# Forty-four stores of a two-layer mixer block issued by ScalarE instead of SyncE

## The chip, the cores and the metric

The kernel runs on one core of one Trainium2 chip. The metric is the device time of one execution in microseconds (us), given as the median of several runs. One further execution is recorded by the hardware profiler, and every row shown here comes from that one.

The core has five instruction streams that matter: TensorE (PE in the rows, with PEld for its weight loads), VectorE (DVE), ScalarE (ACT), GpSimd (POOL) and SyncE (SP). Each works through its own list in order. A "q" behind an engine's name (SPq, ACTq) stands for its sequencer: waits, branches and the issue of transfers (DMAs), which are not counted as busy time.

## The reference, cut to what matters

Two layers (DEPTH 2) of a block on 1024 tokens x of width 1024 beside 256 context tokens. Each layer normalises, projects by `w_in` (1024 x 3856), runs four token mixers on 256 columns each, gates, multiplies by `w_out` and adds to the input. All is float32.

```
h = rms_norm(x, g_pre[l]) * (1 + scale) + shift ; p = h @ w_in[l]        # context alike
a: retention, two directions, 4 heads:   scores = (q k^T) * decay ; o ; head norm ; * silu(z)
b: spatial gating: gelu(u) * (w_s layer_norm(gelu(v)) + b_s) * silu(z)
c: short convolution: b * conv3(c * h) * silu(z)
d: gated delta rule, two directions, 4 heads, chunks of 64:
   q,k,v = silu(conv3(.)) ; q,k l2-normalised ; g = -exp(a_log)*softplus(a + dt) ; beta = sigmoid(b)
   gc = cumsum(g) in a chunk ; decay = exp(gc_i - gc_j)
   (I + lower(k k^T * decay * beta)) u = [v beta, k beta exp(gc)]        # triangular solve
   chunk after chunk: state update and output ; o * rsqrt(mean o^2) * norm_g * silu(z)
x = x + gate * rms_norm(concat(a, b, c, d) @ w_out[l], g_post[l])
```

## The kernel before, in words

Projections are done in three products (high and low halves of both operands) on TensorE. A piece of weights is loaded by SP (`halves`, L507), its high half is cast by ScalarE (`whi`, L511) and its low half is taken by GpSimd (`wlo`, L512), and then TensorE multiplies (`fm_products`, L607 to L609). The next piece of weights is prepared while the present one is multiplied.

Each layer (`run`) first does the gates of the delta rule (`gates`), then walks through its serial stages: `delta_keys`, `lanes`, `delta_queries`, `invert`, `delta_values`, `delta_solve`, `delta_steps`, `delta_out`. Between the steps of these, `beside` puts portions of independent work, a generator of projections and of the other mixers (`fillers`), so that TensorE has something to do while a serial stage waits. `drain` runs the rest of the generator.

Some tensors go through device memory to change their layout. All of these transfers are issued by SP in the kernel before:

- `gates`, L1017: the cumulated gates, turned by TensorE and copied by ScalarE (`ga`), are stored as decay rows `gc`. `delta_keys` (L1077) then loads them spread over partitions into `gR`, 32 loads in all.
- `delta_keys`, L1097: the token-major keys (`gkt`, copied from PSUM by ScalarE) are stored to `ktd`; `delta_solve` loads them back much later.
- `delta_queries`, L1162: the queries (`gp`, a Silu of ScalarE) are stored to `qd`; `delta_out` loads them back.
- `spread`, L778 and L781: the rows of the retention's head norm (`frow`, made by two activations of ScalarE in `rsqrt`, L361 and L362) are stored to `rfd` in four or eight small pieces and loaded back over partitions (L785).
- `delta_gate`, L1502: the Silu of the gate projection (`gz`) is stored to `gzd` in blocks, and `delta_out` loads it (L1482).

The order of the instructions on each engine isn't the order of the code. The framework (a tile scheduler) draws it when the kernel is built, from dependencies, priorities and its own estimates of when an operand is there; it also sets the waits. `after` adds an edge for that order alone, without a wait at run time:

```
self.tc.add_manual_dep(ins.ins, anchor.ins.name, LATER, reason="order")
```

So a transfer that goes to another engine's list can also move other instructions in the lists. In `lanes`, L1186 and L1192, a large relayout through device memory stands next to the stores of the queries. `affine_select` in `delta_keys` (L1082) runs on GpSimd, in the same list as `wlo`.

Of the kernel before, what the change touches and what calls it, by code (L numbers as in the profile page):

```python
# [19 lines left out]
P = 128  # L20
D = 1024
KC = 8
TL = 1024
TC = 256
T = TL + TC
# [68 lines left out]
class Block:  # L94
# [30 lines left out]
    def cst(self, c, n, r=slice(None)):  # L125

        o = max(x for x in self.csts if x <= c)
        return self.csts[o][1][r, c - o:c - o + n]
# [642 lines left out]
    def spread(self, rows, blocks, nm, pool, behind=None):  # L771

        nc = self.nc
        self.uid += 1
        d = self.dp.tile([2, T], F32, name=f"{nm}d{self.uid}")
        for g in range(4):
            if len(blocks) > 1:
                self.after(nc.sync.dma_start(d[:, :TL].rearrange("h (b g i) -> g h b i", b=2, g=4)[g],  # L778
                                             rows[32 * g:32 * g + 2, :256].rearrange("h (b i) -> h b i", b=2)), behind)
            if blocks[-1][0] == TL:  # L780
                self.after(nc.sync.dma_start(d[:, TL + 64 * g:TL + 64 * g + 64], rows[32 * g:32 * g + 2, 256:320]), behind)  # L781
        n = blocks[-1][0] + blocks[-1][1]
        o = self.slot(nm, pool)
        for hh in range(2):
            nc.sync.dma_start(o[64 * hh:64 * hh + 64, :n], d[hh:hh + 1, :n].to_broadcast([64, n]))  # L785
        return o
# [170 lines left out]
    def gates(self, l):  # L957

        nc, cst = self.nc, self.cst
        V = nc.vector  # L960
        tri = self.slot("tri", "G")[:, :C_N - C_TRI]
        self.after(nc.sync.dma_start(tri, self.a["cst"][:, C_TRI:]), self.have_mv)
        w = self.slot("ga", "G")
        x, e, u, ln_, den = (w[:, 160 * j:160 * j + 160] for j in range(5))
        x3 = x.rearrange("p (t k) -> p t k", k=16)
        na = self.small([P, 8], "na", 1)
        V.tensor_tensor(x3[:, :, :8], self.ab[:, :, :8], self.gv[:, 0, l].unsqueeze(1).to_broadcast([P, NT, 8]), ALU.add)
        V.tensor_scalar(x3[:, :, 8:], self.ab[:, :, 8:], -1.0, None, ALU.mult)
        self.log_exp(V.scalar_tensor_tensor(e, x, -1.0, x, ALU.mult, ALU.min))
        have_e = nc.scalar.activation(e, e, AF.Exp)  # L970

        V.tensor_scalar(u, e, 1.0, None, ALU.add)
        nc.scalar.activation(ln_, u, AF.Ln)
        V.tensor_scalar(u, u, -1.0, None, ALU.add)
        V.tensor_scalar(den, u, 0.0, None, ALU.is_equal)
        V.tensor_tensor(ln_, ln_, den, ALU.add)
        V.tensor_tensor(den, u, den, ALU.add)
        V.reciprocal(den, den)
        V.tensor_tensor(ln_, ln_, den, ALU.mult)
        V.tensor_tensor(e, ln_, e, ALU.mult)  # L980
        V.scalar_tensor_tensor(x, x, 0.0, e, ALU.max, ALU.add)
        self.after(nc.scalar.activation(na, self.gv[:, 1, l], AF.Exp), have_e)
        g = w[:, 800:880].rearrange("p (t k) -> p t k", k=8)
        V.scalar_tensor_tensor(g, x3[:, :, :8], -1.0, na.unsqueeze(1).to_broadcast([P, NT, 8]), ALU.mult, ALU.mult)

        pv = self.ps("vt")
        for d in range(2):
            nc.tensor.matmul(pv[:, 40 * d:40 * d + 40], lhsT=tri[:, 128 * d:128 * d + 128], rhs=g[:, :, 4 * d:4 * d + 4],
                             start=True, stop=True)
            nc.tensor.matmul(pv[:, 80 + 80 * d:160 + 80 * d], lhsT=tri[:, 256 + 128 * d:384 + 128 * d], rhs=g,  # L990
                             start=True, stop=True)

        vt = self.held("vtok", [P, NT, 24])
        self.eg = self.held("gexp", [P, NT, 8])
        gk = w[:, 880:960].rearrange("p (k t) -> p k t", t=NT)
        for d in range(2):
            p = pv[:, 40 * d:40 * d + 40].rearrange("p (t h) -> p t h", h=4)
            V.tensor_copy(vt[:, :, 4 * d:4 * d + 4], p)
            nc.scalar.copy(gk[:, 4 * d:4 * d + 4].rearrange("p h t -> p t h"), p)
        V.tensor_scalar(vt[:, :, 16:24], x3[:, :, 8:], -1.0, None, ALU.mult)  # L1000
        for q in range(2):
            r = slice(64 * q, 64 * q + 64)
            V.tensor_tensor(vt[r, :, 8:16], pv[r, 80 + 80 * q:160 + 80 * q].rearrange("p (t k) -> p t k", k=8), vt[r, :, 0:8], ALU.subtract)
        V.tensor_tensor(vt[:, :, 8:16], vt[:, :, 8:16], vt[:, :, 16:24], ALU.add)
        nc.scalar.activation(self.eg, vt[:, :, 0:8], AF.Exp)
        self.vtok = vt

        self.ec = self.held("gec", [P, 2, NT, 8])
        nc.scalar.activation(self.ec.rearrange("p q t k -> p (q t k)"), pv[:, 80:240], AF.Exp)

        pt = self.ps("gcT")
        nc.tensor.transpose(pt[:80, :P], w[:, 880:960], self.ident)
        gr = w[:80, 960:1088]
        self.have_eg = nc.scalar.copy(gr, pt[:80, :P])
        self.uid += 1
        self.gcd = [self.dp.tile([8, T], F32, name=f"gc_{self.uid}")]
        nc.sync.dma_start(self.gcd[0].rearrange("k (t i) -> (k t) i", i=P), gr)  # L1017

    def big(self, cols, nm, bufs=1):
        self.uid += 1  # L1020
# [38 lines left out]
    def delta_keys(self, l):  # L1059

        nc, cst = self.nc, self.cst
# [26 lines left out]
        for hp, k in enumerate(ks):  # L1088
            kt, sq = self.slot("gkt", "G"), self.slot("gks", "G")
            for t0, m in BLOCKS[True]:  # L1090
                self.beside(0.5, 1.5)
                pt = self.ps("gkT")
                for i in range(0, m, P):
                    nc.tensor.transpose(pt[:, i:i + P], k[:, t0 + i:t0 + i + P], self.ident)
                nc.scalar.copy(kt[:, t0:t0 + m], pt[:, :m])
                nc.scalar.activation(sq[:, t0:t0 + m], pt[:, :m], AF.Square)
            nc.sync.dma_start(self.ktd[hp], kt[:, :T])  # L1097
            last = V.tensor_reduce(kk[:, 0, :, 2 * hp:2 * hp + 2], sq[:, :T].rearrange("p (t h d) -> p t h d", h=2, d=64), AX.X, ALU.add)
        lk, self.sk = kk[:, 0], kk[:, 1]
        self.log_exp(last)  # L1100
# [43 lines left out]
    def delta_queries(self, l, ctx):  # L1144

        nc, cst = self.nc, self.cst
        V = nc.vector
        n = T if ctx else TL
        nt = n // P
        qs = self.delta_need(0)  # L1150
        D4 = self.D4

        def use_a(p, h, ts_):
            for d in range(2):
                V.tensor_tensor(D4[d][:, h, ts_], p, D4[d][:, h, ts_], ALU.mult)

        self.uid += 1
        self.qd = self.dp.tile([2, P, T], F32, name=f"qd{self.uid}")
        self.Ad = self.dp.tile([2, P, NT, 4, 64], F32, name=f"Ad{self.uid}")
        pq = self.ps("gq2")  # L1160
        for hp in range(2):
            nc.sync.dma_start(self.qd[hp, :, :n], qs[hp][:, :n])  # L1162
            q2 = self.slot("gq2", "G")
            nc.scalar.activation(q2[:, :n], qs[hp][:, :n], AF.Square)
            for t in range(nt):
                nc.tensor.matmul(pq[:, 20 * hp + 2 * t:20 * hp + 2 * t + 2], lhsT=q2[:, t * P:t * P + P],
                                 rhs=cst(C_INDQ, 2), start=True, stop=True)
            self.gram(self.qkv[1][hp], qs[hp], hp, range(nt), use_a)
        self.fq = self.held("gfq", [P, NT, 4])
        for hp in range(2):  # L1170
            nc.scalar.copy(self.fq[:, :nt, 2 * hp:2 * hp + 2], pq[:, 20 * hp:20 * hp + 2 * nt].rearrange("p (t h) -> p t h", h=2))
        for d in range(2):
            for h in range(4):
                self.after(nc.sync.dma_start(self.Ad[d][:, :nt, h], D4[d][:, h, :nt]), self.have_nl)
# [317 lines left out]
    def delta_gate(self, l, ctx):  # L1492

        nc = self.nc
        self.uid += 1
        zd = self.dp.tile([2, P, T], F32, name=f"gzd{self.uid}")
        for hp in range(2):
            z = self.slot("gz")

            def ev(b, t0, m):  # L1500
                nc.scalar.activation(z[:, t0:t0 + m], b, AF.Silu)
                nc.sync.dma_start(zd[hp, :, t0:t0 + m], z[:, t0:t0 + m])  # L1502

            yield from self.proj_fm(l, 14 * 256 + hp * P, BLOCKS[ctx], ev)
        self.gz = zd
# [181 lines left out]
```

## Time and profile before

| what | value |
|---|---|
| median of 3 runs | 1469.44 us (1469.21 to 1475.08) |
| profiled execution, its own time | 1477.17 us |
| its span, first to last instruction | 1475.4 us |
| mean granted TensorE clock | 0.961 of full speed |
| TensorE busy | 1378.5 us (93%) |
| VectorE, ScalarE, GpSimd busy | 741.5, 450.3, 325.9 us |
| mean DMA traffic | 113 GB/s |

The span leaves out 1.77 us of the profiled execution's own time. Busy time is the union of an engine's instructions; a wait or an issue on a sequencer is not part of it. The table of waits names, for each idle stretch of an engine, the instruction that stood next and what it waited for.

### The profile page before, as it was taken

To read this page: it belongs to the slowest core of one execution; us is meant where nothing else is said; L and a number is where in the kernel's file an instruction comes from. 1 tells how busy PE (TensorE), PEld (TensorE's weight loads), DVE (VectorE), ACT (ScalarE), POOL (GpSimd) and SP (SyncE) were. 2 spreads that over 40 slices of the span, in tenths; PEclk is the share of its full clock that TensorE was granted. 3 is DMA by queue.
4 is the path that set the end of the run, shared out by engine and by line. 5 is a ranking of instruction groups with operands and counts; after the bars stand their busy time and mean duration, and the time that the engine had idled before them with its cause. 6 is when DMAs were issued, how large, how long until landed. Compare 5 with 4: busy or idle time off the path is not lost.

```text
span 1475.4 us, 36425 instructions
## 1 busy us (share of the span) xinstructions
PE 1378.5 (93%) x15928; PEld 1156.9 (78%) x15928; DVE 741.5 (50%) x1385; ACT 450.3 (31%) x930; POOL 325.9 (22%) x265
## 2 busy tenths in 40 slices
PE   5799999799999999999999997997899999999997
PEld 4688788666787777789999985886667867878997
DVE  2477596333335727241555466393553576634232
ACT  5545422121101222322555535312111112333221
POOL 1123231113102211032222035111222112123220
PEclk9899899799999999999999998996999999999999
DMA  9505656126313212373334144644233004136351
GB/s 289 171 16 130 134 142 161 40 88 236 113 58 98 76 51 68 94 246 104 102 123 143 51 94 116 136 111 113 64 113 116 23 27 127 58 108 208 114 180 56
DMA packets 235849, 166.00 MB, mean 113 GB/s; under 512 B 112070, under 2 KB 205610, under 8 KB 235690
## 3 DMA queue, kind: packets, MB, share of 16 engines
q1 hardware_dynamic: 235690, 163.67, 38.3%
q8 instruction: 125, 2.05, 0.6%
q14 instruction: 34, 0.28, 0.1%
HBM read 123.39 MB, written 40.24 MB: 111 GB/s over the span
## 4 chain that ended last, share of the span: by engine, by line
PE 72%; DVE 11%; issue 7%; ACT 4%; DMA 3%; POOL 2%; SPq 0%; DVEq 0%; POOLq 0%; ACTq 0%
PE pj L607 13%; PE pj L608 12%; PE pj L609 12%; PE po L1578 4%; PE po L1580 4%; PE po L1579 4%; PE pt L599 3%; PE pt L601 2%; PE pt L600 2%; PE gu L1368 2%; DVE lt L1210 1%; PE ro L926 1%; POOL wlo L512 1%; PE ip L1253 1%; PE iq L1242 1%
## 5 line engine op out<-in xcount | busy, mean ns | idle before, releaser
L512 POOL TENSOR_TENSOR wlo<-raw,whi 128x512 fp32r<-128x512 f32 (+3 forms) x158 | 217.0, 1388 | 845.9 <-ACT whi L511 719.3
L607 PE MATMUL pj<-h0h,whi 128*128 128x512 f32 (+1 forms) x532 | 211.3, 397 | 8.8 <-ACT whi L511 6.0
L609 PE MATMUL pj<-h0h,wlo 128*128 128x512 f32 (+1 forms) x532 | 203.5, 383 | 3.1 <-POOL wlo L512 3.1
L608 PE MATMUL pj<-h0l,whi 128*128 128x512 f32 (+1 forms) x532 | 203.8, 383 | 0.0
L607 PE MATMUL pj<-h1h,whi 128*128 128x512 f32 (+1 forms) x532 | 203.4, 382 | 0.0
L608 PE MATMUL pj<-h1l,whi 128*128 128x512 f32 (+1 forms) x532 | 199.2, 374 | 0.0
L609 PE MATMUL pj<-h1h,wlo 128*128 128x512 f32 (+1 forms) x532 | 198.2, 373 | 0.1
L1578 PE MATMUL po<-wo,whi 128*128 128x256 f32 x576 | 163.5, 284 | 2.0 <-DVE hf L1604 1.5
L1580 PE MATMUL po<-wo,wlo 128*128 128x256 f32 x576 | 162.0, 282 | 0.8 <-POOL wlo L512 0.8
L1579 PE MATMUL po<-wo,whi 128*128 128x256 f32 x576 | 161.7, 281 | 0.0
L607 PEld LDWEIGHTS pj<-h0h,whi 128*128 128x128 f32 x532 | 104.6, 197 | 29.5 <-ACT whi L511 6.1
L609 PEld LDWEIGHTS pj<-h0h,wlo 128*128 128x128 f32 x532 | 104.0, 196 | 22.3 <-POOL wlo L512 3.8
L608 PEld LDWEIGHTS pj<-h0l,whi 128*128 128x128 f32 x532 | 104.3, 196 | 19.0 <-issue 3.2
L609 PEld LDWEIGHTS pj<-h1h,wlo 128*128 128x128 f32 x532 | 100.9, 190 | 18.9 <-issue 1.0
L607 PEld LDWEIGHTS pj<-h1h,whi 128*128 128x128 f32 x532 | 101.1, 190 | 18.4 <-issue 0.4
L608 PEld LDWEIGHTS pj<-h1l,whi 128*128 128x128 f32 x532 | 101.3, 190 | 17.8 <-issue 1.9
L511 ACT CAST whi<-raw 128x512 fp32r<-128x512 f32 (+3 forms) x158 | 91.4, 608 | 70.0 <-DMA raw<-yd 29.6
L1578 PEld LDWEIGHTS po<-wo,whi 128*128 128x128 f32 x576 | 108.8, 189 | 4.0 <-DVE hf L1604 3.7
L1580 PEld LDWEIGHTS po<-wo,wlo 128*128 128x128 f32 x576 | 108.6, 189 | 1.0 <-POOL wlo L512 1.0
L1579 PEld LDWEIGHTS po<-wo,whi 128*128 128x128 f32 x576 | 108.7, 189 | 0.0
L1604 DVE TENSOR_TENSOR hf<-po,G 128x512 f32<-128x512 f32 x36 | 24.8, 689 | 116.4 <-ACT hg L1602 110.6
L1602 ACT ACTIVATE hg<-po 128x512 f32<-128x512 f32 x36 | 21.5, 598 | 112.9 <-PE po L1580 112.9
(318 smaller groups left out, 2364.6 us busy)
## 6 DMA issues: line engine op xcount, KB each, us to landing
raw<-in_w_in SPq DMA_DIRECT2D x120, 256.0 KB
wm<-in_w_mod SPq DMA_DIRECT2D x64, 256.0 KB
x<-in_x SPq DMA_DIRECT2D x16, 512.0 KB
wq<-in_w_mod SPq DMA_DIRECT2D x8, 1024.0 KB
raw<-yd SPq DMA_DIRECT2D x32, 256.0 KB
gR<-gc SPq DMA_DIRECT2D x32, 160.0 KB
nd<-gR SPq DMA_DIRECT2D x16, 320.0 KB
gR<-Ad SPq DMA_DIRECT2D x18, 256.0 KB
```

The costliest lines, as they stand in the source:

```text
L511: self.nc.scalar.copy(hi, raw)
L512: (engine or self.nc.gpsimd).tensor_tensor(lo, raw, hi.bitcast(F32), ALU.subtract)
L599: nc.tensor.matmul(b, lhsT=ah, rhs=hi, start=(kc == 0), stop=False)
L600: nc.tensor.matmul(b, lhsT=ah, rhs=lo, start=False, stop=False)
L601: nc.tensor.matmul(b, lhsT=al, rhs=hi, start=False, stop=(kc == KC - 1))
L607: nc.tensor.matmul(b[:, :n], lhsT=hi[kc], rhs=self.h(0, kc, t0, n), start=(kc == 0), stop=False)
L608: nc.tensor.matmul(b[:, :n], lhsT=hi[kc], rhs=self.h(1, kc, t0, n), start=False, stop=False)
L609: self.recent = nc.tensor.matmul(b[:, :n], lhsT=lo[kc], rhs=self.h(0, kc, t0, n), start=False, stop=(kc == KC - 1))
L1368: nc.tensor.matmul(pu[half(p), o:o + 64], lhsT=Zc[half(p), s, 2 * hp + h], rhs=four(vtk)[half(p), t, h], start=True, stop=True)
L1578: nc.tensor.matmul(b, lhsT=yh[kc], rhs=self.W[0, kc, j], start=kc == 0 and jj == 0, stop=False, skip_group_check=True)
L1579: nc.tensor.matmul(b, lhsT=yh[kc], rhs=self.W[1, kc, j], start=False, stop=False, skip_group_check=True)
L1580: held = nc.tensor.matmul(b, lhsT=yl[kc], rhs=self.W[0, kc, j], start=False, stop=kc == KC - 1 and jj == 1, skip_group_check=True)
```

## The change

The stores at L778, L781, L1017, L1097, L1162 and L1502 are issued by ScalarE (`nc.scalar.dma_start`) instead of SP (`nc.sync.dma_start`). Sources, destinations, sizes and all loads stay as they are. That is 16 + 8 stores at L778 and L781, 2 at L1017, 4 at L1097, 4 at L1162 and 10 at L1502: 44 in one execution.

```
@@ spread
-                self.after(nc.sync.dma_start(d[:, :TL].rearrange("h (b g i) -> g h b i", b=2, g=4)[g],
+                self.after(nc.scalar.dma_start(d[:, :TL].rearrange("h (b g i) -> g h b i", b=2, g=4)[g],
                                              rows[32 * g:32 * g + 2, :256].rearrange("h (b i) -> h b i", b=2)), behind)
             if blocks[-1][0] == TL:
-                self.after(nc.sync.dma_start(d[:, TL + 64 * g:TL + 64 * g + 64], rows[32 * g:32 * g + 2, 256:320]), behind)
+                self.after(nc.scalar.dma_start(d[:, TL + 64 * g:TL + 64 * g + 64], rows[32 * g:32 * g + 2, 256:320]), behind)
@@ gates
-        nc.sync.dma_start(self.gcd[0].rearrange("k (t i) -> (k t) i", i=P), gr)
+        nc.scalar.dma_start(self.gcd[0].rearrange("k (t i) -> (k t) i", i=P), gr)
@@ delta_keys
-            nc.sync.dma_start(self.ktd[hp], kt[:, :T])
+            nc.scalar.dma_start(self.ktd[hp], kt[:, :T])
@@ delta_queries
-            nc.sync.dma_start(self.qd[hp, :, :n], qs[hp][:, :n])
+            nc.scalar.dma_start(self.qd[hp, :, :n], qs[hp][:, :n])
@@ delta_gate
-                nc.sync.dma_start(zd[hp, :, t0:t0 + m], z[:, t0:t0 + m])
+                nc.scalar.dma_start(zd[hp, :, t0:t0 + m], z[:, t0:t0 + m])
```

## Rows read from the trace of the kernel before

**Rows 1.** The page's table of engines: busy us, share of the span, instructions.

```profile
PE 1378.5 (93%) x15928; PEld 1156.9 (78%) x15928; DVE 741.5 (50%) x1385; ACT 450.3 (31%) x930; POOL 325.9 (22%) x265
```

**Rows 2.** Waits of TensorE: who waited for whom, us in total, times, longest.

```profile
PE pj L607 <- ACT whi L511: 6.0, 1, 6.0
...
PE pj L609 <- POOL wlo L512: 3.1, 1, 3.1
...
PE pj L607 <- DVE wsT L723: 2.5, 1, 2.5
```

**Rows 3.** Waits of SP's queue, same columns.

```profile
SPq L1017 <- ACT base L1009: 71.9, 2, 36.8
...
SPq L778 <- ACT frow L362: 54.0, 4, 18.5
...
SPq L1097 <- ACT gks L1096: 24.7, 4, 9.9
...
SPq L1162 <- ACT gp L1042: 4.9, 1, 4.9
...
SPq L1077 <- DMA gc<-ga: 2.8, 2, 1.7
```

**Rows 4.** Windows: stretch, length, busy us by engine, granted clock, DMA share, GB/s.

```profile
109.00:155.00 46.00, 46.00 (x375) 38.42 (x374) 38.27 (x49) 28.28 (x46) 20.19 (x24) 1.00 0.43 105
...
600.00:630.00 30.00, 30.00 (x180) 24.29 (x179) 4.76 (x9) 11.04 (x20) 5.09 (x4) 1.00 0.41 126
...
885.00:910.00 25.00, 15.86 (x116) 11.77 (x115) 17.41 (x20) 15.85 (x23) 14.01 (x7) 0.73 0.39 123
...
1300.00:1340.00 40.00, 40.00 (x240) 31.62 (x237) 6.91 (x10) 13.31 (x22) 6.92 (x5) 1.00 0.49 150
```

**Rows 5.** SP's queue in order of time, 800 to 960 us: start, length, issue.

```profile
819.70 2.15 SPq L507 DMA_DIRECT2D raw<-in_w_in  x4
858.56 0.33 SPq L1017 DMA_DIRECT2D gc<-ga  x1
860.77 11.81 SPq L1077 DMA_DIRECT2D gR<-gc  x16
872.63 1.53 SPq L507 DMA_DIRECT2D raw<-in_w_in  x2
...
890.88 0.38 SPq L507 DMA_DIRECT2D raw<-in_w_in  x1
```

**Rows 6.** Single lines on SP's queue: duration min/median/max in ns, first and last start.

```profile
L1017 SPq DMA_DIRECT2D gc<-ga x2: 332/332/332, 109.0 to 858.6; - x2
...
L778 SPq DMA_DIRECT2D rfd<-frow x16: 238/254/267, 545.3 to 1313.7; - x16
...
L781 SPq DMA_DIRECT2D rfd<-frow x8: 252/253/262, 545.6 to 611.4; - x8
...
L1097 SPq DMA_DIRECT2D ktd<-gkt x4: 338/340/345, 126.7 to 890.4; - x4
...
L1162 SPq DMA_DIRECT2D qd<-gp x4: 319/536/561, 179.6 to 941.7; - x4
...
L1502 SPq DMA_DIRECT2D gzd<-gz x10: 320/428/695, 613.2 to 1328.8; - x10
...
L507 SPq DMA_DIRECT2D raw<-in_w_in x104: 367/451/4112, 13.1 to 1340.1; - x104
```

**Rows 7.** ScalarE in order of time: start, length, what, idle before it and its releaser.

```profile
547.93 0.58 ACT L838 COPY rk<-pj 128x512 f32<-128x512 f32 x1 [2.19 <-PE pj L609]
...
893.68 0.33 ACT L1101 ACTIVATE base<-base 128x40 f32<-128x40 f32 x1 [1.68 <-DVE base L1098]
...
895.59 0.63 ACT L1042 ACTIVATE gp<-gp 128x513 f32<-128x513 f32 x1
896.13 0.60 ACT L511 CAST whi<-raw 128x512 fp32r<-128x512 f32 x1
```

**Rows 8.** SP's queue and ScalarE around the store of the queries, layer 0.

```profile
168.79 7.79 SPq L1192 DMA_DIRECT2D nl<-nd  x5
...
173.35 2.42 ACT L1164 ACTIVATE gq<-gp 128x1280 f32<-128x1280 f32 x2
```

## The prediction

> **What bounds the kernel now.** I read the table of engines first. TensorE is busy for 1378.5 of 1475.4 us, 93%, and no other engine is above half; ScalarE has 450.3 us of work, 31% [rows 1]. So the kernel is bound by TensorE's work, and a change that touches none of that work can only win back idle time of TensorE: 1475.4 - 1378.5 = 97 us in all. The second view was TensorE's list of waits, to see which part of the 97 us could have to do with a transfer that SP was late with. Nearly all of it stands in places that the change doesn't reach: the loads and norms of the first 80 us, the strings of small products in the triangular inverse, and short waits for VectorE. What stands in or next to the stages that hold the moved stores are three waits: 6.0 us for a cast of weights on ScalarE, 3.1 us for the low half of weights on GpSimd, and 2.5 us for a copy of the spatial weights on VectorE [rows 2]. Together that is 11.6 us, and none of the three is a wait for a transfer.
>
> The third view was SP's own list of waits, which looks quite different: SP stands 71.9 us in front of the gate store L1017, 54.0 us in front of the norm-row store L778, 24.7 us at L1097 and 4.9 us at L1162 [rows 3], some 155 us in which nothing behind the store can be issued. The question is whether anything behind it was late. The windows say that mostly it wasn't: TensorE is busy for 46.00 of 46 us after the first gate store, 30.00 of 30 us around the norm rows and gate blocks of layer 0, and 40.00 of 40 us around those of layer 1 [rows 4]. Only from 885 to 910 us, in `delta_keys` of layer 1, is it busy for just 15.86 of 25 us, at a mean granted clock of 0.73 [rows 4]; the 6.0 and the 3.1 us are there.
>
> **The change, part by part.** *The gate store L1017.* SP waits for it until 858.56 us, issues it, and goes on at 860.77 us with the sixteen loads of the decay rows, which need the store's data [rows 5]; they wait 2.8 us in two layers for its landing [rows 3]. If ScalarE issues the store right behind its copy, SP stands in front of L1077 instead of L1017, until the same moment. What could pass is the two weight loads at 872.63 us, but they are behind L1077 in SP's list, not only behind L1017 [rows 5]. I take a gain of 0.
>
> *The key stores L1097.* SP is held before the second one until shortly before 890.88 us, where a weight load follows [rows 5]. The cast that TensorE waits for at that time is the one at 896.13 us [rows 7]. It is the first cast after the pair of loads at 872.63 us, so its data had been on the way for 23 us; it stands in ScalarE's list behind L1101, which waited 1.68 us for VectorE, and behind a Silu at 895.59 us [rows 7]. So the list order of ScalarE holds it, not SP. Gain 0, as long as that order stays.
>
> *Norm rows and gate blocks.* Their consumers on SP (L785, L1482) need the data of these very stores, and TensorE has full work there [rows 4]. Gain 0; the cover is projections that don't depend on them.
>
> *What is added: issues in ScalarE's list.* No row of before shows a transfer issued by ScalarE, so the price comes from the same stores on SP, line by line at the median: 16 x 0.254 + 8 x 0.253 + 2 x 0.332 + 4 x 0.340 + 4 x 0.536 + 10 x 0.428 = 14.5 us [rows 6]. From below the bound is their shortest, 44 x 0.238 = 10.5 us, and even 0 if the issue runs beside the engine's work. From above it is the longest issue of a weight load, 4.1 us [rows 6], for a store that falls into a full queue; 44 of those would be 181 us, but the ten to sixteen repeats of a moved line never went above 0.695 us, so I take 14.5 us. Waits come on top only for the engine's own last result, since each store reads what ScalarE itself wrote shortly before.
>
> Who stands behind these issues on ScalarE? Evictions of `pj` and casts of `whi`, and behind them TensorE. The longest burst is the eight norm-row stores of layer 0, 4 x 0.254 + 4 x 0.253 = 2.0 us. In the place where it would fall ScalarE has 2.19 us of idle time before the next `pj` copy at 547.93 us [rows 7]. The gate blocks fall into stretches where ScalarE is busy for 11.04 of 30 and 13.31 of 40 us [rows 4]. So these issues cost 0; without that cover they would cost their own 14.5 us, 1%. In the one stretch where TensorE does wait for ScalarE, the second key store (0.34 us) falls into the 1.68 us before L1101 [rows 7] and costs nothing. The first query store of layer 1 reads the Silu of 895.59 us, and if it is put between that and the cast, it delays the cast by its shortest, 0.32 us [rows 6].
>
> **Sum.** On the profiled execution 1477.17 + 0.3 = 1477.5 us. That execution lies 7.73 us (0.5%) above the median of the runs, so against the median 1469.44 + 0.3 = 1469.8 us.
>
> A rule speaks against the change at one place, and it would act where the lists of SP and ScalarE issue at once. Around 170 us SP puts out five pieces of `nl` in 7.79 us, 1.56 us each, and at 173.35 us ScalarE starts the squares of the queries, whose store could stand right before them [rows 8]. If two engines can't issue at the same time, ScalarE would stand for one such piece, 1.56 us, or for what is left of all five, 168.79 + 7.79 - 173.35 = 3.2 us, and TensorE's sums of squares would come later by as much; twice, once in each layer, that is 3.1 to 6.4 us. The Trainium skill (Perfetto Trace Analysis, section "DMA Instruction — HWDGE (DVE, Sync)") says that the unit that makes a transfer's descriptors is locked for one sequencer at a time, and that the wait for this lock is part of the profiled issue. By it the sum would be 1472.6 to 1475.9 us; no row of before can show it, since SP is the only issuer.
>
> **The rivals.**
>
> *Faster: the freed queue mends the stall at 890 us.* The scheduler redraws all lists. With the stores out of SP's list, the weight loads of 872.63 and 890.88 us may be placed, and expected, earlier, and then the cast of 896.13 us may be placed ahead of L1101. Then 6.0 + 3.1 us go, and the time is 1469.4 - 9.1 = 1460.3 us; with the 2.5 us as well it is 1457.8. For it: SP's list is not the order of the code, for four weight loads that come later in the code stand ahead of the gate store at 819.70 us [rows 5]. Against it: the expected time of the loads, not the real wait, moves them, and the loads at 872.63 us stand behind sixteen others that stay on SP.
>
> *Slower: the redrawn order makes such a stall elsewhere.* One mechanism: a cast of weights put behind an instruction on ScalarE that waits for VectorE, as at 893.68 us. The place is `delta_keys` of layer 0, where the same code ran from 109 to 155 us without a gap. The price is what layer 1 pays, 9.1 us: 1478.5 us. It decides as soon as the cast comes after TensorE's last product with the old weights. For it: 44 new instructions in ScalarE's list, four of them in just these stages. Against it: their prices are a third to half a microsecond.
>
> *The change does nothing but pass waits on.* SP waits at L1077, L785 and L1482 for the landing instead of at the store for the data, and ScalarE's issues vanish in its idle time: 1469.4 us.
>
> *Two issuers shut each other out*, as worked out above: 3.1 to 6.4 us, 1472.5 to 1475.8 us, and a second such place would bring it over the bound.
>
> **How the numbers follow.** What a measurement of this kernel can tell from no change is about 0.5%, 7.3 us: faster is below 1462.1, slower above 1476.8 us. The forecast has 0.36, the passing on of waits 0.13, faster by the mended stall 0.24, slower by a new one 0.19, the mutual exclusion 0.08, of which I put half over the bound. Faster 0.24; same 0.36 + 0.13 + 0.04 = 0.53; slower 0.19 + 0.04 = 0.23. The range runs from all 11.6 us back (1458) to a new stall with the smaller exclusion on top (1478.5 + 3.1, cut to 1481), and I leave 2 in 10 outside for an order redrawn in other places. The time is that of the likeliest case, 1469.8 us.
>
> **What would show it.** In the changed kernel's profile, the 44 issues stand on ACTq at 0.24 to 0.7 us each; SP's waits at L1017, L778 and L1097 are gone and waits at L1077 and L785 have grown; TensorE's busy time is 1378 us within a few; the windows after the gate store and around the norm rows are still full. The forecast is wrong if the wait of `pj` for `whi` in `delta_keys` of layer 1 is gone (faster), if one of several microseconds has come up in `delta_keys` of layer 0 or elsewhere (slower), or if issues on ACTq last over a microsecond.

## The result, and the profile after

The changed kernel takes 1485.25 us (median of 4 runs, 1482.57 to 1487.83), the kernel before beside it 1471.2 us (4 runs). The recorded ratio is 1.0079, 95% interval 1.0055 to 1.0104: slower, clear of the noise, by 11.6 us of 1471.2. The two medians themselves are 14.05 us apart; the text goes by the ratio, the smaller figure. 1485.25 us lies above the range of the prediction, which ended at 1481 us. The profiled execution of the changed kernel took 1482.57 us, at a mean granted clock of 0.961, that of before 1477.17 us at the same 0.961. The two profiles are thus only 5.4 us apart, less than the medians, so single traces are used here to find places, and timed pairs to price them.

The table of engines in the page of the changed kernel answers to [rows 1]:

```profile
PE 1380.7 (93%) x15928; PEld 1158.2 (78%) x15928; DVE 741.7 (50%) x1385; ACT 452.0 (31%) x932; POOL 330.1 (22%) x265
```

The work is the same. TensorE's waits, to be held against [rows 2] (who waited for whom, us in total, times, longest):

```profile
PE sgs L753 <- DVE szz L757: 5.0, 2, 4.8
...
PE pj L607 <- DVE gR L1120: 3.9, 2, 2.4
...
PE pj L609 <- POOL wlo L512: 2.1, 1, 2.1
PE pj L607 <- DVE szz L757: 2.0, 1, 2.0
```

The 6.0 us for `whi` and the 2.5 us for `wsT` of [rows 2] are gone. New are waits for VectorE's L757, which reads the products `sgs` of the spatial gating: 4.8 and 2.0 us. New, too, are 3.9 us for its L1120, which e8 below takes up. The windows of the changed kernel say where (columns as in [rows 4]):

```profile
109.00:155.00 46.00, 43.88 (x305) 36.72 (x304) 34.02 (x39) 28.83 (x48) 19.65 (x18) 0.99 0.49 134
229.00:245.00 16.00, 9.27 (x50) 7.50 (x50) 13.40 (x17) 2.01 (x4) 6.41 (x3) 0.79 0.35 98
600.00:630.00 30.00, 30.00 (x216) 23.55 (x210) 6.78 (x13) 9.20 (x17) 2.54 (x2) 1.00 0.30 93
885.00:910.00 25.00, 22.86 (x166) 18.08 (x164) 21.24 (x22) 16.46 (x28) 10.56 (x8) 1.00 0.38 122
1300.00:1340.00 40.00, 40.00 (x276) 31.42 (x275) 9.90 (x19) 12.02 (x20) 5.12 (x4) 1.00 0.39 117
```

The stall of 885 to 910 us has been mended (22.86 us busy for 15.86), and the stretches around the norm rows and gate blocks are full, as they were. From 229 to 245 us, in layer 0, TensorE works for only 9.27 of 16 us. The same window of the kernel before is full:

```profile
229.00:245.00 16.00, 16.00 (x110) 13.61 (x110) 11.41 (x18) 2.18 (x5) 2.45 (x2) 1.00 0.68 121
```

TensorE's list there in the changed kernel, in order of time (start, length, what, idle before it and its releaser):

```profile
234.75 0.47 PE L607 MATMUL pj<-h0h,whi 128*128 128x512 f32 x1 [1.98 <-DVE szz L757]
...
239.98 1.12 PE L753 MATMUL sgs<-wsT,sv 128*64 128x128 f32 x8 [4.76 <-DVE szz L757]
```

1.98 + 4.76 = 6.74 us, which is all of 16 - 9.27 = 6.73 us. VectorE in the same stretch:

```profile
233.25 0.75 DVE L1212 TENSOR_REDUCE xl<-lt 128x42 f32<-128x588 f32 x1
233.93 0.68 DVE L757 TENSOR_TENSOR szz<-sgs,wsT 128x512 f32<-128x512 f32 x1
234.52 1.31 DVE L1210 TENSOR_TENSOR lt<-nl,xl 128x675 f32<-128x675 f32 x1
235.74 0.69 DVE L759 TENSOR_TENSOR szz<-szz,su 128x512 f32<-128x512 f32 x1
236.35 0.85 DVE L1212 TENSOR_REDUCE xl<-lt 128x45 f32<-128x675 f32 x1
237.11 0.99 DVE L742 TENSOR_TENSOR su<-su,szz 128x512 f32<-128x512 f32 x1
238.03 1.30 DVE L1210 TENSOR_TENSOR lt<-nl,xl 128x675 f32<-128x675 f32 x1
239.24 0.68 DVE L757 TENSOR_TENSOR szz<-sgs,wsT 128x512 f32<-128x512 f32 x1
239.84 0.85 DVE L1212 TENSOR_REDUCE xl<-lt 128x45 f32<-128x675 f32 x1
```

VectorE is never idle here. The two reads of `sgs` (L757) stand between the last steps of the triangular inverse (L1210, L1212). In the kernel before, VectorE had ended that inverse 16 us earlier, at 223.98 + 0.86 us, and its first read of `sgs` in this stretch came later than now, not sooner:

```profile
223.98 0.86 DVE L1212 TENSOR_REDUCE xl<-lt 128x45 f32<-128x675 f32 x1
...
239.13 0.68 DVE L757 TENSOR_TENSOR szz<-sgs,wsT 128x512 f32<-128x512 f32 x1
```

So before, TensorE didn't wait for reads that came later still. What makes it wait now is where the products go. PSUM is the memory that TensorE writes its products to, in eight banks, 0 to 7, and the framework that draws the lists also gives each product tile one of them when the kernel is built. In the built programs the tiles of this place have these banks (e3 and e5 are experiments below):

```
tile of layer 0                   before  changed  e3   e5
sgs, first block of 512 tokens    4       1        0    0
sgs, second block of 512 tokens   5       0        1    1
sgs, third block of 256 tokens    6       0        7    6
pj, the projection beside it      7       1        6    5
```

In the changed kernel `pj` reuses the bank of the first `sgs`, and the third `sgs` that of the second, each next after it in that bank. TensorE may not write them before L757 has read the old tile; in the other three, nothing of this stage is left to be read in their banks.

SP's waits in the changed kernel, for [rows 3]:

```profile
SPq L1077 <- DMA gc<-ga: 74.6, 2, 38.4
...
SPq L785 <- DMA rfd<-frow: 64.2, 11, 20.3
...
SPq L507 <- DMA ktd<-gkt: 20.4, 2, 15.7
...
SPq L507 <- DMA qd<-gp: 7.1, 1, 7.1
```

And the stores on ScalarE's queue, line by line, for [rows 6]:

```profile
L1017 ACTq DMA_DIRECT2D gc<-ga x2: 338/351/364, 109.3 to 865.7; - x2
...
L778 ACTq DMA_DIRECT2D rfd<-frow x16: 232/268/488, 552.1 to 1319.3; - x16
...
L781 ACTq DMA_DIRECT2D rfd<-frow x8: 255/266/272, 552.6 to 617.3; - x8
...
L1097 ACTq DMA_DIRECT2D ktd<-gkt x4: 326/326/347, 124.8 to 898.9; - x4
...
L1162 ACTq DMA_DIRECT2D qd<-gp x4: 326/326/329, 143.6 to 924.3; - x4
...
L1502 ACTq DMA_DIRECT2D gzd<-gz x10: 326/326/453, 619.5 to 1334.4; - x10
```

### The profile page after: what moved, and what is told of

Its sections match the earlier page's. It is cut to its first block, busy times and chain, and to the rows that moved or that the text cites. A ratio compares the mean times of both kernels' runs of the same rounds, so it can differ in the third digit from the quotient of the medians.

```text
span 1480.8 us, 36418 instructions
## 1 busy us (share of the span) xinstructions
PE 1380.7 (93%) x15928; PEld 1158.2 (78%) x15928; DVE 741.7 (50%) x1385; ACT 452.0 (31%) x932; POOL 330.1 (22%) x265
## 5 line engine op out<-in xcount | busy, mean ns | idle before, releaser
L512 POOL TENSOR_TENSOR wlo<-raw,whi 128x512 fp32r<-128x512 f32 (+3 forms) x158 | 221.0, 1413 | 859.2 <-ACT whi L511 717.8
```

Source lines behind the costliest of these rows:

```text
L512: (engine or self.nc.gpsimd).tensor_tensor(lo, raw, hi.bitcast(F32), ALU.subtract)
```

## The experiments

The first theories were A, that the new order of the lists costs the time, and B, that the issuing by ScalarE does. Four kernels separate them; each was timed in 5 rounds beside the kernel before. Two of them need a way to hold every engine to a recorded list. It is an edge from each instruction to the one before it, without a wait at run time:

```
+    for names in ORDER.values():
+        for before, n in zip(names, names[1:]):
+            tc.add_manual_dep(here[n], before, LATER, reason="pin")
```

Such edges change more than the order. The framework's estimates change with them, and it gives out the banks of PSUM, and the places of tiles in SBUF, the memory that holds the operands, anew: in the built programs 7% of the matmul instructions have another bank in e2 than in the kernel before, and 10 to 11% in e3, e5 and e9 than in the kernel whose lists they hold. Two pairs are free of this: e6 differs from e5, and e7 from e3, by two waits alone, with the same lists, banks and places.

### e1: the late stores alone

Only the norm rows (L778, L781) and the gate blocks (L1502) move, 34 of 44 stores:

```
-                self.after(nc.sync.dma_start(d[:, :TL].rearrange("h (b g i) -> g h b i", b=2, g=4)[g],
+                self.after(nc.scalar.dma_start(d[:, :TL].rearrange("h (b g i) -> g h b i", b=2, g=4)[g],
...
-                nc.sync.dma_start(zd[hp, :, t0:t0 + m], z[:, t0:t0 + m])
+                nc.scalar.dma_start(zd[hp, :, t0:t0 + m], z[:, t0:t0 + m])
```

> Only the 34 late stores (norm rows at L778 and L781, gate blocks at L1502) are issued by ScalarE; the lists of TensorE, VectorE and GpSimd stay instruction for instruction as before. Theory A (the loss comes from the redrawn order of the lists): ratio to the kernel before 1.000, within 0.003. Theory B (the loss comes from issuing on ScalarE, 14.5 us of issues, and from what queues behind them): 34 of 44 stores and 10.3 of 14.5 us, so 1.005 to 1.007.

Measured: 1471.72 us, ratio 1.000 (0.9984 to 1.0016). The lists of TensorE, VectorE and GpSimd stay as they were, and the 34 issues cost nothing that can be measured.

### e2: all stores on ScalarE, in the order of before

The changed kernel with the lists of the kernel before:

```
     Block(ctx, tc, a, dbg).run(out, **k)
+    pin(tc)
```

> All 44 stores on ScalarE, but every engine's list is held in the order of the kernel before by edges without a wait. Theory A: 1.000, within 0.003, since the order is what costs. Theory B: 1.007 to 1.009 as in the changed kernel, and SP's waits for the landing of the key and query stores (18 us in layer 0 of the changed kernel) are there as well.

Measured: 1474.29 us, ratio 1.0016 (1.0000 to 1.0033). The issuing of all 44 stores by ScalarE is not where the 0.8% comes from. Theory B falls. This holds although SP's unrelated weight loads wait for the landing of the key stores in e2 too:

```profile
SPq L507 <- DMA ktd<-gkt: 17.6, 2, 12.7
```

### e3: all stores on SP, in the order of the changed kernel

The kernel before with the lists of the changed one, by the same edit.

> All 44 stores on SP as before, but every engine's list is held in the order of the changed kernel. Theory A: 1.007 to 1.009, with the wait of TensorE for the spatial gating near 235 us and the first inversion step near 190 us as in the changed kernel. Theory B: 1.000, within 0.003.

Measured: 1476.12 us, ratio 1.0021 (1.0001 to 1.0041). So the order by itself isn't it either, and theory A falls in this form. The trace shows what is missing: the third `sgs`, in the same place of the same list, starts with no wait.

```profile
233.85 0.66 PE L753 MATMUL sgs<-wsT,sv 128*64 128x128 f32 x8
```

### e4: the early stores alone

Gates, keys and queries (L1017, L1097, L1162), 10 of 44 stores:

```
-        nc.sync.dma_start(self.gcd[0].rearrange("k (t i) -> (k t) i", i=P), gr)
+        nc.scalar.dma_start(self.gcd[0].rearrange("k (t i) -> (k t) i", i=P), gr)
...
-            nc.sync.dma_start(self.ktd[hp], kt[:, :T])
+            nc.scalar.dma_start(self.ktd[hp], kt[:, :T])
...
-            nc.sync.dma_start(self.qd[hp, :, :n], qs[hp][:, :n])
+            nc.scalar.dma_start(self.qd[hp, :, :n], qs[hp][:, :n])
```

> Only the 10 early stores (gates L1017, keys L1097, queries L1162) on ScalarE; the lists are redrawn as in the changed kernel. Theory A: 1.007 to 1.009, the whole loss from 10 of 44 stores. Theory B by issues: 4.2 of 14.5 us, so 1.002 to 1.003; by waits for landings it would be near 1.008 too, which e2 tells apart.

Measured: 1484.7 us, ratio 1.0080 (1.0057 to 1.0103): the whole loss, from ten issues. The waits for L757 are there (5.5 and 2.0 us), and its program has the banks 1, 0, 0 and 1 of the changed kernel, as it has all its other banks. With e3, which has the same order on TensorE but other banks at this place, this led to theory C: the time is lost where a bank is given out again while a late reader still needs it. Theory D kept the rest: issuing and order cost only together.

### e5: the changed kernel and its order, with other banks

The changed kernel, held to its own lists. The edges change the framework's estimates, and the banks come out anew (table above).

> The changed kernel (all 44 stores on ScalarE) with every engine's list held to the list of the changed kernel itself, by edges that wait for nothing. With these edges the framework estimates other times and gives out other banks of PSUM: the third tile sgs of layer 0's spatial gating and the projection pj beside it get banks whose last tile was read long before, where in the changed kernel they take the banks of the first two tiles sgs, which VectorE's line 757 still has to read. Theory C (the time is lost in those two bank waits, 2.0 and 4.8 us of idle TensorE near 233 us, and some 2 us of the like in layer 1): no idle time by DVE szz L757 near 233 us, ratio about 1.002 (0.999 to 1.005), as e3. Theory D (the stores on ScalarE and the new lists cost only when both are there, since e2 and e3 had one each): ratio about 1.008, as the changed kernel.

Measured: 1477.51 us, ratio 1.0029 (1.0007 to 1.0050). The stretch that lost 6.74 us is full, at the full clock (its window, and the third `sgs`):

```profile
231.00:247.00 16.00, 16.00 (x87) 13.22 (x86) 15.68 (x19) 2.70 (x5) 5.85 (x3) 1.00 0.23 76
...
236.00 0.66 PE L753 MATMUL sgs<-wsT,sv 128*64 128x128 f32 x8
```

### e6: the same, with the two waits put back

The banks are those of e5; the first matmuls of `pj` and of the third `sgs` (I-2287, I-2265) wait for L757's reads of the first and the second `sgs` (I-2249, I-2261), as in the changed kernel:

```
+    for matmul, read in (("I-2287", "I-2249"), ("I-2265", "I-2261")):
+        tc.add_manual_dep(here[matmul], read, wait, reason="bank")
```

> e5 with one thing more: the first matmul of that projection pj and of the third tile sgs wait for VectorE's line 757 to read the first and the second tile sgs, the counts of the semaphore that they wait for in the changed kernel; the banks stay those of e5. Theory C: idle TensorE of 2 and 5 us by DVE szz L757 near 233 us is back, and the ratio is some 0.005 above that of e5, at 1.006 to 1.009 (about 7 us of 1470 in layer 0; what layer 1 loses in the changed kernel is not put back). Theory D: as e5, near 1.008 both.

Measured: 1483.2 us, ratio 1.0077 (1.0052 to 1.0102). Two waits bring back 1.0077 - 1.0029 = 0.0048, or 7.1 us of 1472.05, for 1.94 + 5.63 = 7.57 us of idle TensorE; the medians of the two, timed side by side, are 1483.2 - 1477.51 = 5.7 us apart. The mean granted clock over all their runs is 0.963 in e5 and 0.964 in e6, so that the difference isn't one of clock from run to run. The window of e6 and its two waits:

```profile
229.00:245.00 16.00, 8.43 (x44) 6.85 (x43) 13.76 (x17) 2.11 (x4) 5.79 (x3) 0.69 0.33 95
...
234.33 0.47 PE L607 MATMUL pj<-h0h,whi 128*128 128x512 f32 x1 [1.94 <-DVE szz L757]
...
240.43 1.12 PE L753 MATMUL sgs<-wsT,sv 128*64 128x128 f32 x8 [5.63 <-DVE szz L757]
```

### e7: the two waits with no store on ScalarE

e3 and the same two edges.

> The kernel before, all its stores on the common transfer queue, with the lists of the changed kernel (e3, 1.0021) and those two waits. Nothing of the change itself is in it but what it did to the plan. Theory C: idle TensorE by DVE szz L757 of some 7 us near 233 us, ratio about 1.007 (1.005 to 1.010). Theory D: nothing is issued by ScalarE, so about 1.002, as e3.

Measured: 1485.22 us, ratio 1.0087 (1.0054 to 1.0120), beside 1.0021 of e3: 0.0066 for the two waits, or 9.7 us, where e6 gave 0.0048. The two sets of runs are from different sessions, and the six runs of e7 had a lower mean clock, 0.960 for 0.964 in e3, so the figure of e6 is the better price. The loss of the change can be had without the change.

```profile
239.40 0.47 PE L607 MATMUL pj<-h0h,whi 128*128 128x512 f32 x1 [2.01 <-DVE szz L757]
...
245.39 0.91 PE L753 MATMUL sgs<-wsT,sv 128*64 128x128 f32 x6 [5.53 <-DVE szz L757]
```

Theory D falls: e5 has both parts of it and isn't slow by 0.8%, e7 has only one and is.

### e8: all but the queries

40 stores on ScalarE; L1162 stays on SP.

> The change without its four stores of queries: 40 of 44 stores on ScalarE, no edge added, the framework free to plan. The lists come out new (the stores of keys alone redraw over 500 of TensorE's lines), but by the program's PSUM addresses the third tile sgs gets bank 5 and the projection bank 6, where nothing is left to be read. Theory C: no wait for DVE szz L757 near 233 us, ratio within 0.4% of 1.000. Theory D, or any theory by which the number of stores on ScalarE or a redrawn list costs: 1.005 to 1.008.

Measured: 1482.31 us, ratio 1.0060 (1.0035 to 1.0085). The forecast by theory C, within 0.4% of 1.000, was wrong. There is indeed no wait for L757 near 233 us, but another one in layer 1. TensorE and then VectorE, in order of time:

```profile
919.60 0.40 PE L609 MATMUL pj<-h1h,wlo 128*128 128x512 f32 x1
919.92 0.45 PE L1139 MATMUL gram<-gp 64*64 64x64 f32 x14
924.60 0.77 PE L607 MATMUL pj<-h0h,whi 128*128 128x512 f32 x1 [4.22 <-DVE gR L1120]
...
926.87 0.63 PE L609 MATMUL pj<-h0h,wlo 128*128 128x512 f32 x1
...
921.97 3.27 DVE L1120 TENSOR_TENSOR gR<-gram,gR 128x512 f32<-128x512 f32 x8
```

In the program of e8 this `pj` has bank 0, whose last tile is one of the two products `gram` just written, and L1120 is their reader. The changed kernel has the same reuse at this place, with a wait of 2.4 us at 914.27 us. The expectation had rested on the banks of one place, and the plan had made the same mistake at another.

### e9: the same order, with other banks

e8 held to its own lists. The `pj` gets bank 4, whose last tile was an older `gram`.

> e8 (1.006) with every engine's list held to e8's own, so that the banks are given out anew and nothing else. In e8 a projection pj of layer 1 takes bank 0 of PSUM while VectorE's line 1120 still has to read the tile gram in it (TensorE idle 4.2 us at 920 us, then matmuls at a granted clock of 0.57 in 925 to 930 us); here it gets bank 4, whose tile was read before. Theory C, made general (what costs is a bank that is given out while a late reader still needs it, wherever the plan puts one): no wait of pj for gR L1120 of over 1.5 us, ratio 1.000 to 1.004. Theory E (e8 loses by the order of its lists, by the low half wlo at 996 us for one, 4.5 us, and the bank is not it): 1.005 to 1.007 again.

Measured: 1474.18 us, ratio 1.0014 (0.9994 to 1.0034), against 1.0060. Since other banks changed with that of the `pj`, this supports the bank as the cause in e8 and doesn't isolate it, as e5 and e6 do for the changed kernel. Theory E's candidate, the 4.51 us for the low half at 996 us, is gone as well, but only in name: in e8 it stands beside 2.42 us for L1232, 6.93 us in all, and in e9 there is one wait of 7.83 us for L1232 in the same place. So that place doesn't make the difference. The windows of this place, e8 and then e9:

```profile
915.00:935.00 20.00, 15.78 (x128) 12.03 (x128) 10.21 (x19) 7.23 (x10) 7.66 (x7) 0.83 0.47 99
```

```profile
915.00:935.00 20.00, 20.00 (x121) 16.17 (x113) 8.09 (x16) 8.51 (x11) 2.69 (x3) 1.00 0.93 174
```

### e10: layer 0 in the old order, layer 1 in the new one

All stores on SP; a try at a faster version, with neither the waits near 233 us nor the stall of 885 to 910 us.

> A try at a version faster than both: all stores on the common transfer queue, layer 0 in the order of the kernel before, layer 1 in that of the changed kernel, whose layer 1 lacks the 9.1 us stall at 890 us. Theory C: no bank wait near 233 us, no 6.0 us wait for whi L511 at 890 us; against that stand waits of the new layer 1 seen in e3 and e5 (1.7 to 4.2 us near 890 to 920 us, 2.3 to 2.7 us more at L1242), so a ratio of 0.996 to 1.000. If the stall at 890 us is worth nothing (its 9.1 us come back whole at later waits): 1.000 to 1.002.

Measured: 1469.87 us beside 1472.17, ratio 0.9989 (0.9972 to 1.0006): not to be told from no change. The windows suggest why, e10 and then the kernel before, from 910 us on:

```profile
885.00:910.00 25.00, 24.49 (x182) 18.70 (x180) 20.29 (x22) 16.58 (x28) 12.84 (x8) 1.00 0.38 122
910.00:1015.00 105.00, 93.87 (x1106) 78.12 (x1106) 69.63 (x123) 29.04 (x47) 24.09 (x18) 0.92 0.57 128
```

```profile
910.00:1015.00 105.00, 99.42 (x1076) 82.13 (x1076) 67.10 (x120) 28.01 (x46) 20.81 (x16) 0.95 0.58 130
```

From 885 to 910 us e10 has 24.49 - 15.86 = 8.63 us more work done [rows 4], and in the next 105 us it has 99.42 - 93.87 = 5.55 us less. By these two traces most of the mended stall is given back at later waits; no pair of runs prices it.

## Why the prediction was wrong

**The step that failed** is the sum: 1469.4 + 0.3 us, in which nothing stands for what the redrawing itself costs. The text said "Gain 0, as long as that order stays" and then summed as if it stayed. The order didn't stay, and with it went the banks. Two terms were missing. The two bank waits cost 0.0048, 7.1 us (e6 against e5); the new order with the stores on ScalarE costs about 0.0029, 4.3 us (e5). Their sum, 11.4 us, is no more than e6's own ratio, 1.0077, beside 1.0079 of the changed kernel, and the agreement is in part luck, since e6 doesn't put back the wait of 2.4 us at 914 us. The first term is shown from both sides: the time comes down without the waits (e5) and goes up with them, with nothing else changed (e6, and e7 without a store on ScalarE). Of the second, e3 measures 0.0021 with the stores on SP. Both intervals reach down nearly to zero, and where those few microseconds are is not settled. It is a net figure, since the wait of 6.0 us for `whi` is gone in e3 and e5 too. In e10, with layer 0 in the old order and layer 1 in the new one, nothing of it is left (0.9989). That points to layer 0, but e3 and e10 were run in different sessions and their banks differ, so it isn't shown.

**The slower rival** had the right kind, a redrawn order that makes a stall elsewhere, with 9.1 us as its price and a chance of 0.19. Its mechanism and place were wrong: not a cast on ScalarE behind an instruction that waits for VectorE in `delta_keys`, but TensorE waiting for a bank of PSUM in the spatial gating. The range ended where it did because it allowed for one new stall of 9.1 us and a small one. The measured loss needs the bank waits and the cost of the rest of the new order.

**The faster rival** came true in its place and not in the time. The wait for `whi` near 890 us is gone, as it said, and by its mechanism: the two weight loads of 872.63 us stand ahead of the decay loads now, in a row of six, and the two casts long before L1101, which starts at 902.59 us (SP's queue, then ScalarE):

```profile
825.53 4.77 SPq L507 DMA_DIRECT2D raw<-in_w_in  x6
...
880.11 1.14 ACT L511 CAST whi<-raw 128x512 fp32r<-128x512 f32 x2
```

The parts on L1017 and L1097 had ruled this out by the order of SP and of ScalarE before, and that order was redrawn. But the rival took the 9.1 us for a gain in the end time. In e10, which has this gain and no bank wait near 233 us, 0.0011 is left (1.6 us), and at most 0.0028 (4.1 us).

**The cost of issuing** was right. The 44 issues sum to 2 x 0.351 + 16 x 0.268 + 8 x 0.266 + 4 x 0.326 + 4 x 0.326 + 10 x 0.326 = 13.0 us at the medians, for 14.5 predicted, and they cost nothing that can be told from noise where the order stays (e1 1.000; e2 1.0016, whose interval begins at 1.0000). The 0.3 us of the sum had nothing to act on: the casts stand at 880.11 us, the first query store of layer 1 at 911.62 us. Nor do the issues save anything, in agreement with the Trainium skill (DMA: Bandwidth & Descriptors, "Issuing engines are not separate DMA queues"): a second issuing engine saves only the issuing engine's own time.

**The waits of SP** moved as said: 71.9 us at L1017 became 74.6 us at L1077, 54.0 us at L778 became 64.2 us at L785 [rows 3]. What wasn't foreseen are waits of weight loads for key and query stores; e2 has the former, 17.6 us, at a ratio of 1.0016.

**The windows** around norm rows and gate blocks stayed full, as said. The one after the first gate store did not (43.88 of 46 us), by a wait of 2.1 us for `wlo` that e3 shows too, at 1.9 us.

**Two issuers shutting each other out** isn't seen. The second query store of layer 0 was issued in 0.33 us at 165.46 us, while SP was in a row of issues, seven of them from 157.54 us on (start, length, issue; ScalarE's queue, then SP's):

```profile
165.46 0.33 ACTq L1162 DMA_DIRECT2D qd<-gp  x1
...
157.54 13.52 SPq L1186 DMA_DIRECT2D nd<-gR  x7
```

On average one of those seven takes 13.52 / 7 = 1.93 us, and the longest of all 44 issues on ScalarE 0.488 us. The lock that the Trainium skill (Perfetto Trace Analysis, "DMA Instruction — HWDGE (DVE, Sync)") describes is not seen as a longer issue here.

## What to carry to other kernels

When a framework draws lists and gives out buffers from its own estimates, moving ten transfers to another engine can change the whole plan (e4), while moving 34 others left three engines' lists as they were (e1). Before the moved instructions are priced, a chance belongs to the redrawn plan, and it can be the larger term: here the issues cost nothing measurable and the plan 0.8%. Compare the built programs, not only the code: the order of each engine and the bank of each product tile, above all where a reader stands in a long chain of VectorE.

To split such a result, hold the lists fixed and move the transfers, then move the lists and hold the transfers. If neither shows the loss, something else came with the plan; a wait that is put back alone prices it. Holding the lists isn't neutral, since the buffers are given out anew with it.

## What was not expected of the hardware

A single wait can slow the work behind it for some microseconds. After the 4.22 us at 920 us in e8, the rows above show the same matmul of 128x512 at 0.63 us where it took 0.40 us before the wait. From 925 to 930 us its window gives a granted clock of 0.57, near the lower level of 1.2 GHz; from 915 to 935 us it is 0.83 on average, and 1.00 in e9 without the wait. The starts show it too: the six matmuls from 926.87 us on start 0.42 us apart, and from 929.38 us on it is 0.23 us.

```profile
929.38 0.39 PE L609 MATMUL pj<-h0h,wlo 128*128 128x512 f32 x1
929.61 0.39 PE L607 MATMUL pj<-h1h,whi 128*128 128x512 f32 x1
```

The two waits of e6 bring 0.69 from 229 to 245 us, where e5 has 1.00 in its window of the same stage. In the time of the whole kernel this doesn't stand out: those two waits cost 7.1 us for 7.57 us idle, and the intervals of e5 and e6 are too wide to tell the clock's part. From run to run the clock does stand out: in the 27 runs of the kernel before that were taken beside e5 to e8 (1466.36 to 1481.49 us) its mean goes from 0.957 to 0.970, and a line fitted through them gives 1.2 us less for each 0.001 more, with a correlation of -0.80.

The weight loads on SP that wait 20.4 and 7.1 us for the landing of stores with which they have nothing to do are a price of a second issuer that no list of instructions shows. The built program of the changed kernel shows the tie: it counts all these transfers on eight semaphores (counters that instructions wait on), and each of the three loads counts on the one of the store that it waits for, and waits for the store's count first. What this costs is open; no run here takes it apart, and e2 has 17.6 us of it at 1.0016.
